# Two pooling projections computed as an eighth pair of seven block products, six left among the heads

## The chip, the cores and the metric

The kernel runs on one core of one Trainium2 chip. The metric is the device time of one execution in microseconds (us); of several runs the median is taken. The reader meets five engines of the core: PE (TensorE, the matrix unit, with its weight loads shown apart as PEld), DVE (VectorE), ACT (ScalarE), POOL (GpSimd) and SP (SyncE, which here only starts DMA transfers). Each engine takes its instructions in the order in which they stand in its own program, and an instruction waits on semaphores that other engines or DMA transfers raise.

## The reference

One layer of a streaming encoder on 512 tokens, model width 2048, eight heads of 128 channels, four pooling groups of 256 channels, feed-forward width 5632:

```python
h = rms_norm(x, pre_mix_g[l])
z = h @ w_in[l]
q = z[..., :ATTN_WIDTH].reshape(B, S, N_HEADS, HEAD_DIM)
k = z[..., ATTN_WIDTH:2 * ATTN_WIDTH].reshape(B, S, N_HEADS, HEAD_DIM)
v = z[..., 2 * ATTN_WIDTH:3 * ATTN_WIDTH].reshape(B, S, N_HEADS, HEAD_DIM)
u = z[..., 3 * ATTN_WIDTH:]
a = chunked_attention(q, k, v, rel_bias[l]).reshape(B, S, ATTN_WIDTH)
p = multiscale_pool(u, pool_w[l], pool_scale[l])
m = jnp.concatenate([a, p], axis=-1) @ w_o[l]
x = x + rms_norm(m, post_mix_g[l])
h = rms_norm(x, pre_ffn_g[l])
up = causal_dwconv(h @ w_up[l], conv_w[l], conv_b[l])
y = (jax.nn.gelu(up[..., :D_FF], approximate=True) * up[..., D_FF:]) @ w_down[l]
x = x + rms_norm(y, post_ffn_g[l])
```

The pooling takes u, 1024 channels: group g (256 channels) is averaged over a trailing window of 2, 4, 8 or 16 tokens, the token itself is subtracted, and the result goes through a 256x256 map and a scale per channel. The change concerns where the first 256 channels of u are computed, and when their pooling is done.

## The kernel before

**Numbers and tiles.** Activations lie transposed, channels on the 128 partitions and the 512 tokens along the row. Every float32 operand is split into a high part and a low rest (`split`: ACT rounds to the high part at L140, DVE subtracts at L141), and a product is three matmuls: high by high, high by low, low by high (`mm3`, L162, L164, L165). PE is where most of the time goes; its order is the order of the code, laid out by hand. The orders of DVE, ACT, POOL and SP are laid out by a scheduler when the program is built, from the same code.

**Stages, in us from the start of the span.** To 73: q and k of head 0, the first half of v. 73 to 205: q and k of heads 1 to 7, one head after the other (the "pairs"). 205 to 267: heads 0, 1, 2 among the second half of v. 267 to 388: the pooling projections u0 to u7 with heads 3 to 7 among them. 388 to about 545: the output projection. From there to the end: the feed-forward part.

**The pairs** (class `Pairs`, L440; `qk_product`, `qk_keep`). The q block and the k block of a head, two blocks of 128 output channels over 2048 input channels, are cut into halves of the input channels and of the tokens; the two by two product of blocks is made with seven block products instead of eight, in the order 1, 2, 5, 3, 6, 7, 4. Each of them is eight 128x512 matmuls (L170) and eight 128x256 matmuls (L176) through `mm2`. The weights come in four raw tiles of 128x1024 per pair (`load`, from `w_qk`); sums of raw tiles are made by DVE (L476 to L482), and each is split by ACT and DVE. The two 128x512 results of a pair go to DRAM as `zqk[h]` (L583).

**The heads.** `ready_head(h)` multiplies the reloaded pair `zq` by RR (the norm factors, with the sign of the second block turned, L668) and splits it into `qkh`, `qkl`; `scores(h)` is 12 matmuls on PE into `s`, then a softmax on DVE and ACT in four row blocks: scale and bias (L699), maximum (L702), exponential (ACT, L704), reciprocal (L706), scaling (L707). `turn(h)` transposes it on PE (L718, ten matmuls into `pt`) and splits the transposed tiles; `values(h)` multiplies by v. For heads 0 to 2 the loop `for h in range(3)` puts steps of the second half of v between these (`run`, 12 matmuls each).

**The pooling.** `project` computes one block u*j* with 48 matmuls of 128x512 from two weight tiles `u_0`, `u_1`; halfway through it a step of a head can be put in (`between`, made by `mid`). `pool_keep` (L732) multiplies the block by the norm factors (L736), makes the window sums (L740, as `us`), divides and subtracts (L745 to L748, as `tmp`), and splits the result (`dh`, `dl`). `pool_mix` (L750) is the 256x256 map: 12 matmuls into `pm`, stored to DRAM as `pooled` (L771) and later loaded again into `mixT` (L831).

**Queues and buffers around the change.** SP starts loads in its own order, each after the buffer it writes has been let go. `raw4` is a ring of five raw tiles of 128x1024 float32, `w4` a ring of eight split tiles (four pairs), and PSUM, where PE writes, has eight banks. At the end of the pairs, after block product 7 of the last pair, `restore` runs, and then `zq0` (the reloaded pair of head 0, L606) and `bias0` (L608) are started, both in `raw4` tiles. `more_sums(n)` starts DMA sums of feed-forward weights on POOL's queue, paced through these stages.

Of the kernel before, what the change touches and what calls it, by code (L numbers as in the profile page):

```python
# [9 lines left out]
F32 = mybir.dt.float32  # L10
# [5 lines left out]
P = 128  # L16
S = 512
# [4 lines left out]
HEADS = 8  # L22
# [59 lines left out]
def encoder_layer(ctx: ExitStack, tc: tile.TileContext, x, xT, vecs, rel, post_mix, post_ffn,  # L82
# [192 lines left out]
    specs += v_specs(1)  # L275
    for g in range(4):
        specs += u_specs(2 * g)
        if g:
            specs += pm_spec(g - 1)
        specs += u_specs(2 * g + 1)  # L280
# [98 lines left out]
    vd = [dram.tile([P, NT, 512], F32, name=f"vd{i}") for i in range(2)]  # L379
    pooled = dram.tile([P, 6, S], F32, name="pooled")  # L380

    z0 = raw4("z0").rearrange("p (a b) -> p a b", a=2)
# [58 lines left out]
    class Pairs:  # L441
# [3 lines left out]
        def __init__(self):  # L445
            n = self.n = HEADS - 1
            place_of = {1: 0, 2: 2, 5: 4, 3: 6, 6: 8, 7: 10, 4: 12}
            begin = [(0, 1), (0, 2), (0, 5), (1, 1), (0, 3)]
            order = [(k, i) for _, k, i in sorted((7 * k + at, k, i) for k in range(n) for i, at in place_of.items())]
            self.order = begin + [at for at in order if at not in begin]  # L450
            self.order.insert(-2, (None, None))
            self.raw, self.made, self.loaded, self.used = {}, [], 0, 0

        def load(self, k, i):
            def raw(what, tile_, m, kh):
                load_w.last = nc.sync.dma_start(tile_, w_qk[k + 1, m, kh]).ins
                self.raw[k, what] = tile_
# [99 lines left out]
    def qk_keep(k, i):  # L557
# [18 lines left out]
        elif i == 4:  # L576
# [5 lines left out]
            nc.vector.tensor_add(z[:, 0, T:], a[:, :T], z[:, 0, T:])  # L582
            nc.sync.dma_start(zqk[k + 1], z)  # L583

# [8 lines left out]
    for k, i in [at for at in pairs.order if at[0] is not None]:  # L593
# [9 lines left out]
        if (k, i) == (pairs.n - 1, 7):  # L603
            restore()
            state["z", 0] = raw4("zq0").rearrange("p (a b) -> p a b", a=2)
            nc.sync.dma_start(state["z", 0], zqk[0])  # L606
            state["bias", 0] = raw4("bias0")[:, :S]
            restore.last = nc.sync.dma_start(state["bias", 0], rel[0]).ins  # L608
        if i in (3, 7, 4) and k < pairs.n - 1:
            more_sums(1)  # L610
# [10 lines left out]
    with tc.tile_pool(name="p1", bufs=2, reuse_waits="tile") as p1:  # L621
# [21 lines left out]

        def project(name, between=None):
            ps = bank(name)
            for i in range(2):
                if i and between:
                    between()
                w = weights.get(f"{name}_{i}")
                for j in range(8):  # L650
                    kb = 8 * i + j
                    mm3(ps, part(w, j), g_both(hT, kb), kb == 0, kb == KD - 1)
            return ps
# [77 lines left out]

        def pool_keep(g, j, ps):  # L732
            w = WINDOWS[g]
            u = p1.tile([P, WIDE], F32, tag="u", bufs=1, name="u")[:, :PAD + S]
            nc.vector.memset(u[:, :PAD], 0.0)
            nc.vector.tensor_mul(u[:, PAD:], ps, R)  # L736
            cur, step = u, 1
# [40 lines left out]
        for h in range(3):  # L778
# [11 lines left out]
            run(1)  # L790
            ready_head(h + 1)
            run(1)
            turn(h)
# [5 lines left out]
        def mid(h):  # L799
            def step():  # L800
                values(h)
                if h == 2:
                    scores(3)
                elif h + 2 < HEADS:
                    ready_head(h + 2)
# [4 lines left out]

        for j in range(8):
            ps = project(f"u{j}", mid(2 if j == 0 else j + 1) if j not in (1, 7) else None)
            if j == 0:
                ready_head(4)
            if j == 2:
                v_ready()
            if 1 <= j <= 5:
                turn(j + 2)
                if j < 5:
                    scores(j + 3)  # L820
            if j in (2, 4, 6):
                pool_mix(j // 2 - 1, spill_mix)
# [998 lines left out]
```

## Time and profile before

| | us |
|---|---|
| median of three runs | 1853.03 |
| lowest, highest of the three | 1850.68, 1853.16 |
| the profiled execution | 1848.83 |
| its span | 1847.1 |
| PE busy | 1836.0 (99%) |
| DVE busy | 1465.3 (79%) |
| ACT busy | 1123.2 (61%) |
| POOL busy | 310.2 (17%) |

The span is what the profiler's records cover; the execution's own time is 1.7 us longer. A matmul's busy time of 0.39 us is not its cost: matmuls are pipelined, and a 128x512 matmul follows the one before it by about 0.23 us. A row of the timeline reads: start, busy time, engine, line, operation, out<-in by the program's names (numbers left out), shape, count, and in brackets how long the engine was idle before it and what ended that.

### The profile page before, as it was taken

The page shows a single profiled execution, that of the slowest core. Times are in us where ns is not written, and L with a number is a line of the kernel's source. Part 1 is how long each engine was busy: PE and PEld are TensorE (multiplying, and loading weights), DVE is VectorE, ACT ScalarE, POOL GpSimd, SP SyncE. Part 2 cuts the span into 40 slices and gives each one's busy share as a digit, 9 for nine tenths or more (in the row PEclk, how much of TensorE's full clock was granted, in tenths as well). Part 3 has the DMA queues.
Part 4 walks back from the last instruction along what each step waited for, and adds up shares of the span by engine and source line. Part 5 has one row for each costly group of instructions (what it writes and reads, how often), then busy time and mean ns, then how long its engine had stood idle before and what let it go on. Part 6 is the DMA issues. An engine that isn't in the chain of part 4 may idle for free.

```text
span 1847.1 us, 25323 instructions
## 1 busy us (share of the span) xinstructions
PE 1836.0 (99%) x9530; PEld 1577.9 (85%) x9530; DVE 1465.3 (79%) x1702; ACT 1123.2 (61%) x1486; POOL 310.2 (17%) x411
## 2 busy tenths in 40 slices
PE   9999999999999999999999999999999999999998
PEld 7888888888888888888888888888888888888886
DVE  6988778878679887777777777777777899899876
ACT  7655555457587666666666666666665655655553
POOL 3411000100001222222122222221221001111101
PEclk9999999999999999999999999999999999999999
DMA  8599978998979988988889888888888977787785
GB/s 320 173 319 301 319 228 234 277 262 305 336 283 283 248 211 206 208 198 202 206 205 198 204 201 207 195 208 206 203 175 303 360 216 166 195 217 175 176 243 145
DMA packets 139467, 430.21 MB, mean 233 GB/s; under 512 B 12048, under 2 KB 15504, under 8 KB 133648
## 3 DMA queue, kind: packets, MB, share of 16 engines
q0 software_dynamic: 56016, 177.75, 47.3%
q1 hardware_dynamic: 83328, 250.84, 38.6%
q8 instruction: 75, 1.23, 0.3%
q14 instruction: 48, 0.39, 0.1%
HBM read 374.54 MB, written 104.33 MB: 259 GB/s over the span
## 4 chain that ended last, share of the span: by engine, by line
PE 93%; DMA 3%; issue 1%; DVE 1%; ACT 1%; SPq 0%; POOL 0%; DVEq 0%; POOLq 0%; ACTq 0%
PE qa L170 19%; PE qa L176 10%; PE qg L170 9%; PE qg L176 5%; PE qd L170 5%; PE pa L165 4%; PE pa L164 4%; PE pa L162 4%; PE qd L176 2%; PE m L164 2%; PE m L162 2%; PE m L165 2%; PE pg L165 2%; PE pg L164 2%; PE pg L162 2%; PE v L165 2%
## 5 line engine op out<-in xcount | busy, mean ns | idle before, releaser
L170 PE MATMUL qa<-gT,wfh 128*128 128x512 f32 x1200 | 300.4, 392 | 0.0
L141 DVE TENSOR_TENSOR wfl<-x,wfh 128x1024 fp32r<-128x1024 f32 x165 | 202.0, 1225 | 94.8 <-ACT wfh L140 78.9
L170 PEld LDWEIGHTS qa<-gT,wfh 128*128 128x128 f32 x1200 | 215.9, 189 | 38.7
L140 ACT ACTIVATE wfh<-x 128x1024 fp32r<-128x1024 f32 x165 | 174.3, 1056 | 79.8 <-PE qg L170 45.9
L1118 POOL DMA_DIRECT2D x<-in_w_up x125 | 107.2, 860 | 477.0 <-DVE wfl L141 461.6
L176 PE MATMUL qa<-gT,wfl 128*128 128x256 f32 x1200 | 168.0, 283 | 0.7 <-ACT m L1446 0.6
L176 PEld LDWEIGHTS qa<-gT,wfl 128*128 128x128 f32 x1200 | 157.8, 191 | 5.4 <-ACT m L1446 0.8
L170 PE MATMUL qg<-h,wfh 128*128 128x512 f32 x656 | 162.1, 389 | 0.0
L141 DVE TENSOR_TENSOR wfl<-wy,wfh 128x1024 fp32r<-128x1024 f32 x100 | 122.0, 1222 | 33.8 <-ACT wfh L140 31.7
L170 PEld LDWEIGHTS qg<-h,wfh 128*128 128x128 f32 x656 | 123.0, 188 | 25.4
L140 ACT ACTIVATE wfh<-wy 128x1024 fp32r<-128x1024 f32 x100 | 105.1, 1053 | 64.3 <-PE qd L170 49.8
L140 ACT ACTIVATE bh<-b 128x2048 fp32r<-128x2048 f32 x56 | 106.1, 1914 | 62.1 <-DVE b L1245 24.1
L141 DVE TENSOR_TENSOR bl<-b,bh 128x2048 fp32r<-128x2048 f32 x56 | 127.1, 2286 | 18.6 <-ACT bh L140 11.7
L162 PE MATMUL pa<-bh,ah 128*128 128x512 f32 x320 | 124.5, 389 | 0.0
L164 PE MATMUL pa<-bl,ah 128*128 128x512 f32 x320 | 124.5, 389 | 0.0
L165 PE MATMUL pa<-bh,al 128*128 128x512 f32 x320 | 124.5, 389 | 0.0
L170 PE MATMUL qd<-gT,wfh 128*128 128x512 f32 x400 | 99.1, 390 | 0.0
L176 PEld LDWEIGHTS qg<-h,wfl 128*128 128x128 f32 x656 | 89.5, 190 | 6.4
L176 PE MATMUL qg<-h,wfl 128*128 128x256 f32 x656 | 91.5, 282 | 0.0
L170 PEld LDWEIGHTS qd<-gT,wfh 128*128 128x128 f32 x400 | 74.7, 188 | 15.3
L170 PE MATMUL qa<-h,wfh 128*128 128x512 f32 x344 | 86.1, 392 | 0.0
L141 DVE TENSOR_TENSOR wfl<-wz,wfh 128x1024 fp32r<-128x1024 f32 x50 | 61.1, 1223 | 28.8 <-PE qa L170 26.8
(576 smaller groups left out, 4275.5 us busy)
## 6 DMA issues: line engine op xcount, KB each, us to landing
x<-in_w_up POOLq DMA_DIRECT2D x125, 512.0 KB, 6.1
b<-in_w_down SPq DMA_DIRECT2D x32, 1024.0 KB, 6.9
wt<-in_w_o POOLq DMA_DIRECT2D x24, 1024.0 KB, 14.9
wz<-in_w_up SPq DMA_DIRECT2D x43, 512.0 KB, 5.5
x<-in_w_up SPq DMA_DIRECT2D x43, 512.0 KB, 5.0
wy<-in_w_up SPq DMA_DIRECT2D x43, 512.0 KB, 3.9
wy<-in_w_up POOLq DMA_DIRECT2D x43, 512.0 KB, 6.6
sum<-part POOLq DMA_DIRECT2D x38, 512.0 KB, 6.8
```

The source lines that it names most:

```text
L140: rounded = nc.scalar.activation(hi, src, AF.Copy)
L141: rest = nc.vector.tensor_sub(lo, src, f32(hi))
L162: nc.tensor.matmul(ps, l[0], r[0], start=first, stop=False, skip_group_check=onto)
L164: nc.tensor.matmul(low, l[0], r[1], start=False, stop=False, skip_group_check=onto)
L165: nc.tensor.matmul(ps, l[1], r[0], start=False, stop=last, skip_group_check=onto)
L170: nc.tensor.matmul(ps, w[0][:, kb], pairs[kb][0], start=fresh and not kb, stop=last, skip_group_check=not fresh)
L176: nc.tensor.matmul(ps[:, sl], w[1][:, kb], pair[:, sl], start=False, stop=last, skip_group_check=not fresh)
L1118: nc.gpsimd.dma_start(self.raw[k, what], self.block(k, m, kh), accum_op=ALU.add)
```

## The change

The list of pairs gets blocks of its own: (loader of weights, place of the result). The first two channel blocks of the pooling weights are put in as pair number 4 of now eight, between those of heads 4 and 5; the result goes to a new DRAM tensor `zu`. The weight list loses the tiles of u0 and u1, and `pm0` stands ahead of `u2` in it. After `bias0`, a third `raw4` tile `zur` is loaded from `zu`. In the loop of heads 0 to 2, head 0 does `pool_keep` on the first half of `zur`, head 1 on the second, with the factors of `RR` since the second block carries the turned sign, and head 2 does `pool_mix(0)`. The projections left are u2 to u7. `project` takes a table from input block to step: inside u2 stand `scores(3)` and `ready_head(4)` after 4 of 16 input blocks and `values(2)` after 10; the later heads move one projection on in number, so that the last head's `values(7)` stands in the middle of u7, where it stood in the middle of u6.

```diff
-    for g in range(4):
+    specs += pm_spec(0)
+    for g in range(1, 4):
         specs += u_specs(2 * g)
-        if g:
+        if g > 1:
             specs += pm_spec(g - 1)
         specs += u_specs(2 * g + 1)
...
+    zu = dram.tile([P, 2, S], F32, name="zu")
...
-            n = self.n = HEADS - 1
+            self.blocks = [(lambda m, kh, h=h: w_qk[h, m, kh], zqk[h]) for h in range(1, HEADS)]
+            self.blocks.insert(4, (lambda m, kh: w_u[m, kh], zu))
+            n = self.n = len(self.blocks)
...
-                load_w.last = nc.sync.dma_start(tile_, w_qk[k + 1, m, kh]).ins
+                load_w.last = nc.sync.dma_start(tile_, self.blocks[k][0](m, kh)).ins
...
-            nc.sync.dma_start(zqk[k + 1], z)
+            nc.sync.dma_start(pairs.blocks[k][1], z)
...
             restore.last = nc.sync.dma_start(state["bias", 0], rel[0]).ins
+            state["zu"] = raw4("zur").rearrange("p (a b) -> p a b", a=2)
+            nc.sync.dma_start(state["zu"], zu)
...
-        def project(name, between=None):
+        def project(name, between):
             ps = bank(name)
             for i in range(2):
-                if i and between:
-                    between()
+                if 8 * i in between:
+                    between[8 * i]()
                 w = weights.get(f"{name}_{i}")
                 for j in range(8):
                     kb = 8 * i + j
+                    if j and kb in between:
+                        between[kb]()
                     mm3(ps, part(w, j), g_both(hT, kb), kb == 0, kb == KD - 1)
...
-        def pool_keep(g, j, ps):
+        def pool_keep(g, j, ps, r=R):
...
-            nc.vector.tensor_mul(u[:, PAD:], ps, R)
+            nc.vector.tensor_mul(u[:, PAD:], ps, r)
...
             ready_head(h + 1)
+            if h < 2:
+                pool_keep(0, h, state["zu"][:, h], RR[:, h, :])
+            else:
+                pool_mix(0, spill_mix)
             run(1)
             turn(h)
...
-                if h == 2:
-                    scores(3)
-                elif h + 2 < HEADS:
+                if 2 < h < HEADS - 2:
                     ready_head(h + 2)
...
+        def first_scores():
+            scores(3)
+            ready_head(4)
+
-        for j in range(8):
-            ps = project(f"u{j}", mid(2 if j == 0 else j + 1) if j not in (1, 7) else None)
-            if j == 0:
-                ready_head(4)
-            if j == 2:
+        for j in range(2, 8):
+            ps = project(f"u{j}", {8: mid(j)} if j > 2 else {4: first_scores, 10: mid(j)})
+            if j == 3:
                 v_ready()
-            if 1 <= j <= 5:
-                turn(j + 2)
-                if j < 5:
-                    scores(j + 3)
-            if j in (2, 4, 6):
+            if j < 7:
+                turn(j + 1)
+            if j < 6:
+                scores(j + 2)
+            if j in (4, 6):
                 pool_mix(j // 2 - 1, spill_mix)
```

The orders on the engines change at three places that matter below. In the rows, lines of the kernel after stand 4 to 8 higher than those of before for the same statement. What an engine's row waits for stands in brackets as the semaphore's name: DMAHW a DMA transfer, PE, DVE, Activation, Pool that engine.

DVE, at the start of head 0, before (`zq_2037` is `zq0`, `bias_2039` is `bias0`, `s_1` to `s_3` are PE's score banks):

```order
L668 TENSOR_TENSOR zq_2037<-zq_2037,RR 128x1024 [waits DMAHW1_49]
L141 TENSOR_TENSOR qkl<-zq_2037,qkh 128x1024 [waits Activation_49]
L141 TENSOR_TENSOR v_1l<-v_1r,v_1h 128x1024 [waits DMAHW7_49,PE_49,Activation_49]
L689 MEMSET bias_2039 64x64 [waits DMAHW2_49]
L699 SCALAR_TENSOR_TENSOR s<-s_1_2188,bias_2039 128x128 [waits DVE_49,PE_49]
```

And of the change, the same stretch:

```order
L676 TENSOR_TENSOR zq_2221<-zq_2221,RR 128x1024 [waits DMAHW6_49]
L744 TENSOR_TENSOR u<-zur,RR 128x512 [waits DMAHW2_49]
L748 TENSOR_TENSOR us<-u 128x527 [waits DVE_49]
L141 TENSOR_TENSOR qkl<-zq_2221,qkh 128x1024 [waits Activation_49]
L753 TENSOR_TENSOR uf<-us,recip 128x16 [waits DVE_49,Pool_49]
L756 SCALAR_TENSOR_TENSOR tmp<-us,u 128x496
L141 TENSOR_TENSOR v_1l<-v_1r,v_1h 128x1024 [waits DMAHW4_49,PE_49,Activation_49]
L697 MEMSET bias_2223 64x64 [waits DMAHW7_49]
L755 TENSOR_TENSOR tmp<-uf,u 128x16 [waits DVE_49]
L743 MEMSET u 128x16 [waits DVE_49]
L744 TENSOR_TENSOR u<-zur,RR 128x512
L141 TENSOR_TENSOR dl_2475<-tmp,dh_2474 128x512 [waits Activation_49]
```

The multiplication of `zur` by RR, which waits for the new load, and the first window sum now stand between the multiplication of `zq0` and the row that makes `qkl`; five more rows of the pooling stand between `qkl` and the softmax, whose first row (scale and bias) comes right behind the last row shown.

SP, where head 0's loads are started, before:

```order
L606 DMA zq_2037<-zqk_350 128x1024 [waits DMAHW2_49,DMAHW1_49,DVE_49]
L608 DMA bias_2039<-in_rel 128x512 [waits DMAHW4_49,DVE_49,Activation_49]
L658 DMA bias<-in_rel 128x512 [waits DMAHW3_49,PE_49]
L658 DMA bias<-in_rel 128x512
L152 DMA v_2r<-in_w_v 128x1024 [waits DMAHW5_49,DVE_49]
```

And of the change:

```order
L610 DMA zq_2221<-zqk_350 128x1024 [waits DMAHW7_49,DMAHW6_49,DVE_49]
L612 DMA bias_2223<-in_rel 128x512 [waits DMAHW1_49,DVE_49,Activation_49]
L666 DMA bias<-in_rel 128x512 [waits DMAHW0_49,PE_49]
L666 DMA bias<-in_rel 128x512
L614 DMA zur<-zu 128x1024 [waits DMAHW2_49,DVE_49]
L152 DMA v_2r<-in_w_v 128x1024 [waits DMAHW3_49,DVE_49]
```

The load of `zur` stands fifth, where `v_2r` stood, in the ring place that `v_2r` had; what both wait for on DVE is the end of `v_7l`, the split of the weight tile that held that place. `v_2r` comes one later.

PE, at the end of the loop of heads 0 to 2, before (`v_3h` is a weight tile of v, `v_2`, `v_3` are banks, `u_2655` is the bank of u0):

```order
L162 MATMUL v_3_1974<-v_3h,gT_136 128x512
L164 MATMUL v_3_1974<-v_3l,gT_136 128x512
L165 MATMUL v_3_1974<-v_3h,gT_136 128x512
L718 MATMUL pt_0_2626<-ident,s 128x128 x4
L718 MATMUL pt_1_2627<-ident,s 128x128 x4
L718 MATMUL pt_2_2628<-ident,s 128x128 x2
L162 MATMUL u_2655<-gT_135,u_0h 128x512
```

And of the change, the step ahead of that same last step of v:

```order
L162 MATMUL pm_1_2843<-dh_2474,pm0h 128x512
L164 MATMUL pm_1_2843<-dl_2475,pm0h 128x512
L165 MATMUL pm_1_2843<-dh_2474,pm0l 128x512
L162 MATMUL pm_1_2843<-dh_2660,pm0h 128x512
L164 MATMUL pm_1_2843<-dl_2661,pm0h 128x512
L165 MATMUL pm_1_2843<-dh_2660,pm0l 128x512
L162 MATMUL v_0_2155<-v_3h,gT_136 128x512
```

The twelve matmuls of `pool_mix(0)`, of which the last six are shown, moved from the middle of the projections to a place ahead of the last step of v in the loop; after the transposes of head 2 comes u2 where u0 was.

## The prediction

> **What bounds the kernel now.** I read the page first: the busy times and the clock by slices.
>
> ```profile
> PE 1836.0 (99%) x9530; PEld 1577.9 (85%) x9530; DVE 1465.3 (79%) x1702; ACT 1123.2 (61%) x1486; POOL 310.2 (17%) x411
> PEclk9999999999999999999999999999999999999999
> ```
>
> PE is busy for 1836.0 of 1847.1 us at full granted clock, so time falls only if PE gets less to do, and rises wherever PE is made to wait. What there is to gain is decided by PE's work, what there is to lose by how close the other engines run behind it. So next the windows by stage (start:end, length, then busy time of PE, PEld, DVE, ACT, POOL, the clock, the DMA share and GB/s):
>
> ```profile
> 105.00:124.50 19.50, 19.50 (x114) 17.23 (x113) 17.63 (x23) 10.97 (x14) 1.87 (x6) 1.00 1.06 352
> 205.00:267.00 62.00, 62.00 (x313) 52.84 (x312) 48.04 (x101) 34.22 (x66) 3.07 (x8) 1.00 0.84 274
> 267.00:388.00 121.00, 121.00 (x601) 103.01 (x600) 95.01 (x224) 60.46 (x115) 16.02 (x30) 1.00 0.92 254
> 320.00:342.00 22.00, 22.00 (x114) 18.93 (x113) 20.24 (x52) 12.21 (x25) 4.22 (x8) 1.00 1.00 252
> ```
>
> PE never waits in a pair (first row), in the heads with v (second) or in the projections (third). DVE is at 17.63 of 19.50 in that pair and at 20.24 of 22 in the densest piece of the projections (fourth): it has little to spare, and that is where a rearrangement can hurt.
>
> **What the change removes on PE.** The timeline of PE gives the length of a pair and of a projection.
>
> ```profile
> 104.91 0.86 PE L170 MATMUL qa<-gT,wfh 128*128 128x512 f32 x3
> 182.88 0.63 PE L170 MATMUL qa<-gT,wfh 128*128 128x512 f32 x2
> ...
> 282.24 0.39 PE L162 MATMUL u<-gT,u_0h 128*128 128x512 f32 x1
> 293.12 0.93 PE L718 MATMUL pt<-ident,s 128*128 128x128 f32 x7
> ```
>
> The first two rows are the same place in pairs that lie four apart: 182.88 - 104.91 = 77.97, or 19.49 us for a pair. The second two are the start of u1, whose 48 matmuls stand alone, and the first instruction behind it: 293.12 - 282.24 = 10.88 us. Two projections, 21.76, become one pair, 19.49: **2.27 us less on PE**, 0.12% of the whole. The pair brings its own splits, sums and loads, but the rows of seven pairs show that PE waits for none of them, and its weights are the bytes that u0 and u1 loaded. New are a store and a load of 512 KB. Nothing else can be won: the same matmuls of heads, v and pooling map are in both.
>
> **What it puts in the way of head 0.** The order of DVE has `pool_keep(0, 0)` begin ahead of `qkl`, the split that the scores of head 0 need. The stretch before, from DVE, ACT and PE:
>
> ```profile
> 215.06 1.22 DVE L141 TENSOR_TENSOR v_7l<-v_7r,v_7h 128x1024 fp32r<-128x1024 f32 x1
> ...
> 220.04 1.23 DVE L668 TENSOR_TENSOR zq<-zq,RR 128x1024 f32<-128x1024 f32 x1 [1.29 <-DMA zq<-zqk]
> 222.39 1.22 DVE L141 TENSOR_TENSOR qkl<-zq,qkh 128x1024 fp32r<-128x1024 f32 x1 [1.13 <-ACT qkh L140]
> 223.54 1.22 DVE L141 TENSOR_TENSOR v_1l<-v_1r,v_1h 128x1024 fp32r<-128x1024 f32 x1
> ...
> 225.28 0.62 DVE L699 SCALAR_TENSOR_TENSOR s<-s,bias 128x128 f32<-128x128 f32 x2 [0.46 <-PE s L165]
> ...
> 230.16 1.23 DVE L141 TENSOR_TENSOR v_2l<-v_2r,v_2h 128x1024 fp32r<-128x1024 f32 x1 [1.04 <-ACT v_2h L140]
> ...
> 233.61 0.49 DVE L707 TENSOR_SCALAR s<-s,rs 128x512 f32<-128x512 f32 x1
> ```
>
> ```profile
> 224.37 0.28 PE L162 MATMUL s<-qkh 128*128 128x256 f32 x1
> 234.49 1.26 PE L718 MATMUL pt<-ident,s 128*128 128x128 f32 x10
> ```
>
> `qkl` is done at 223.61 and PE takes up the scores at 224.37: 0.8 us to spare. The softmax is done at 234.10 and the transposes begin at 234.49; only the fourth of ten reads the last row block, 3 x 0.1 us on, so 0.7 us to spare. All times here are in the time of before; in the changed kernel the whole stretch lies a pair later.
>
> Now `zur`. Its load takes the place of `v_2r` on SP and in the ring, and both wait for the end of `v_7l`, at 216.28. The rows of SP, and the landing times of loads of the same size (512 KB), of `v_2r`, of `zq`, and of `u_1r`:
>
> ```profile
> 206.69 0.33 SPq L606 DMA_DIRECT2D zq<-zqk  x1
> ...
> 216.31 0.33 SPq L152 DMA_DIRECT2D v_2r<-in_w_v  x1
> 216.69 0.42 SPq L663 DMA_DIRECT2D zq<-zqk  x1
> ```
>
> ```profile
> DMA to landing us min/median/max: 7.8/7.8/7.8
> ```
>
> ```profile
> DMA to landing us min/median/max: 4.4/8.6/13.3
> ```
>
> ```profile
> DMA to landing us min/median/max: 3.9/5.9/8.0
> ```
>
> `v_2r` took 7.8 us from 216.31. The three `zq` are those started at 206.69 (13.3: it gave DVE its wait until 220.04), at 216.69 (8.6) and at 235.9 (4.4). I take 7.8, the load in the same place: `zur` is there at 216.31 + 7.8 = 224.1. The bounds are 3.9 and 13.3. What I can't see is how the sums on POOL's queue, which stand differently ahead of it, share the DMA engines.
>
> From the landing, DVE does the multiplication and one window sum before `qkl`. The rows of those, and of the rest of `pool_keep`, from the groups of the projection stage:
>
> ```profile
> L736 DVE TENSOR_TENSOR u<-u,RR 128x512 f32<-128x512 f32 x8 | 5.5, 688 | 12.0 <-PE u L165 12.0
> L740 DVE TENSOR_TENSOR us<-u 128x527 f32<-128x527 f32 x8 | 5.5, 694 | 0.1
> L748 DVE SCALAR_TENSOR_TENSOR tmp<-us,u 128x496 f32<-128x496 f32 x7 | 4.7, 668 | 0.0
> L141 DVE TENSOR_TENSOR dl<-tmp,dh 128x512 fp32r<-128x512 f32 x7 | 4.8, 683 | 0.6 <-ACT dh L140 0.6
> ```
>
> Each holds DVE for some 0.6 us (a row overlaps its follower by under 0.1: 222.39 + 1.22 against 223.54). So `qkl` ends at 224.1 + 1.2 + 1.2 = 226.5, and PE waits from 224.37: **about 2.2 us at the scores**. Then DVE has, ahead of the softmax, `uf` 0.1, `tmp` 0.6, `v_1l` 1.15, three small rows 0.2, the second block's multiplication 0.6 and `dl` 0.6, 3.3 in all: the softmax starts at 229.8 instead of 225.28. It took 234.10 - 225.28 = 8.8 us, and gets 1.4 more of pooling (`us`, `uf`, `tmp` of the second block), which fits into gaps of 1.04 ahead of `v_2l` and about 0.5 in an earlier gap, all but some 0.3: done at 238.9. That is 4.8 late, less the 0.7 to spare: **4.1 us for head 0**, 2.2 at the scores and 1.9 at the transposes. In short the delay is the landing minus 220.0, and since DVE isn't through with `zq0` before 221.27, it doesn't fall below 1.2 on this order, however early `zur` is.
>
> At this place I weigh a rule. The Trainium skill, page "DMA: Bandwidth & Descriptors", section "Anatomy of one DMA — SWDGE (gpsimd) path", fits a DMA's time as about 2.0 us plus its bytes over 436 per ns, which for 512 KB would be an estimate of 3.2 us; by it `zur` would be there at 219.5 and the delay would be its least, 1.2 instead of 4.1. The two rows at this very place, 7.8 and 8.6, don't agree with it, and I stay with them.
>
> **What it puts in the way later.** Head 1: its transposes had 0.35 to 0.4 to spare, by
>
> ```profile
> 249.76 0.49 DVE L707 TENSOR_SCALAR s<-s,rs 128x512 f32<-128x512 f32 x1
> 250.43 1.26 PE L718 MATMUL pt<-ident,s 128*128 128x128 f32 x10
> ```
>
> (end 250.25, with the fourth transpose again later); `dl` of block 1 comes into that stretch with 0.7 and a split of the pooling weights stands where a wider one of u0 stood. Between 0 and 0.7, and I take 0.1, since the weight split takes most of it away. In the dense piece (20.24 of 22) a head now stands one projection earlier by name, with the same work around it: 0 to 0.5, I take 0.1; not below nothing, since PE doesn't wait there now. `mixT` is the third. Its load of the stored pooling results waits for the last head's output; the row of who waited, and the landing times of the pooled tiles:
>
> ```profile
>   DVE mixT L939: 4.9, 1
> ...
> DMA to landing us min/median/max: 5.8/7.3/11.0
> ```
>
> DVE waited 4.9 us for it, and PE didn't notice. Now `values(7)` stands in u7 rather than u6, so the load starts nearly a projection later, still ahead of the output projection's second factor. DVE's order has splits of output weights behind that wait: nothing at 5.8, about 1.2 at 11.0. I take 0.4. The weights' sums on POOL are paced by as many calls less one; it is off PE's way, and I take nothing, with 0.3 to either side.
>
> **The sum.** -2.27 + 4.1 + 0.1 + 0.1 + 0.4 = +2.4 us. The profiled execution took 1848.83 (span 1847.1), so 1851.2 in its terms. That execution is 4.2 us under the median of the three runs, 1853.03, so by the median **1855.4**.
>
> **The rivals.**
>
> *`zur` is early.* If the queue is emptier when `zur` starts (`u_1r`, 15 us later, took 3.9), it lands by 221.2 and head 0 costs 1.2. With the other terms near nothing that is -2.27 + 1.2 = -1.1: 1851.9. For it speaks that the sums running in that stretch stand otherwise than before; against it, that three loads between 206 and 217 took 7.8 to 13.3. The skill's fit above stands on this side.
>
> *`zur` is late: slower.* If it takes 13.3 like `zq0`, the last reload from DRAM ahead of it, it lands at 229.6, and head 0 waits 9.6: -2.27 + 9.6 + 0.6 = +7.9, or 1861.0. The mechanism is one: DVE stands at the multiplication of `zur`, with `qkl` behind it. It makes the kernel slower by more than 0.2% (3.7 us, about what a measurement of this kernel can tell from no change) once the wait reaches 5.4, that is from a landing of 9.1 us on. For it: `zq0` is a reload from DRAM, as `zur` is; against it: the next reload, in the same queue 0.4 us behind `v_2r`, took 8.6. In this case PE would stand for 7.7 us at once, and a clock row matters:
>
> ```profile
> 1838.00:1839.00 1.00, 0.75 (x7) 0.54 (x5) 0.76 (x4) 0.38 (x2) 0.00 (x0) 1.00 0.03 8
> 1843.00:1844.00 1.00, 0.00 (x0) 0.00 (x0) 0.60 (x2) 0.00 (x0) 0.00 (x0) 0.53 1.03 367
> ```
>
> After PE's last work, in the slice from 1838, the granted clock holds until about 1843 and then falls to half: some 4.3 us of standing. The waits of the forecast, 2.2 and 1.9 with scores between them, stay under that; 7.7 does not, and would cost up to half of the work done until the clock is back, which no row here shows. The Trainium skill, page "TensorE: Matmul & The Clock Gate", section "Part 1: The HAM clock gate", has the clock halved after an idle window of about 3.4 us and released after as much busy time, by which this case would be an estimated 1.7 us slower still, 1862.7; the row above agrees with the fall.
>
> *The dense places give way too.* Head 0 as forecast, and the three later terms at their upper ends, 0.7 + 0.5 + 1.2: -2.27 + 4.1 + 2.4 = +4.2, 1857.3. For it: DVE at 92% in the dense piece; against it: each has its own slack in before, and PE waits nowhere there.
>
> That the change doesn't do what it says I leave out: the eighth pair is the same code as the seven.
>
> **How the numbers follow.** Forecast 0.45, `zur` early 0.25, late 0.15, dense places 0.15. The predicted time is the forecast's, 1855.4. The range reaches from 1850.2, which leaves out the lower end of the early case (all of 2.27 gained, 1850.8, and a little luck), to 1861.0, which leaves out the upper part of the late one. The bound of 3.7 us gives 1849.3 and 1856.7: faster 0.06 (from the early case alone, by the spread of runs, 1850.68 to 1853.16), slower 0.32 (the late case, most of the dense one, and a sixth of the forecast), within 0.62.
>
> **What the profile after would show.** A pair more of 19.5 us with no wait of PE in it, and projections of 10.9 behind it. At head 0, a wait of DVE at the multiplication of `zur`, ended by its DMA; a wait of PE of about 2.2 at the scores, ended by DVE's `qkl`, and one of about 1.9 at the first transposes, ended by DVE's scaling. The landing of `zur` near 7.8. If PE waits nowhere at head 0, the forecast is wrong and the early case holds; if it waits for 5 or more at the scores, the late one. If PE waits at the transposes of heads 1 to 5, or at the output projection for a split of its weights, the later terms were too small. If the eighth pair is longer than 19.5, the gain was wrong.

## The result, and the profile after

| | before | after |
|---|---|---|
| median of the runs on one chip, us | 1852.38 (4 runs) | 1861.63 (4 runs) |
| lowest to highest, us | 1850.68 to 1853.16 | 1858.88 to 1862.47 |
| ratio, 95% interval | | 1.0053 [1.0041, 1.0065] |
| the profiled execution, us | 1848.83 | 1858.88 |
| its span, us | 1847.1 | 1857.1 |

The kernel became slower by 9 us, 0.5%, where the forecast was 1855.4 and the range ended at 1861.0. The first page of the profile after: busy time and share by engine, and PE's granted clock.

```profile
PE 1836.4 (99%) x9546; PEld 1577.9 (85%) x9546; DVE 1474.9 (79%) x1716; ACT 1129.5 (61%) x1494; POOL 311.1 (17%) x413
PEclk9999999989999999999999999999999999999999
```

PE's busy sum hardly moved: the 2.27 us that the pair saves are about what slow matmuls at a low clock add (2.5, below). One slice of the clock, the ninth (371 to 418 us), now shows an 8. The waits of PE in the profile after (what PE waited for, total us, times, longest):

```profile
PE m L162 <- ACT wo_3h L140: 6.2, 1, 6.2
PE m L164 <- DVE wo_3l L141: 1.9, 1, 1.9
PE pt L726 <- DVE s L715: 1.1, 1, 1.1
PE pd L162 <- ACT ah L140: 1.1, 1, 1.1
...
PE pd L165 <- DVE al L141: 0.5, 1, 0.5
```

None of these five is among the waits of before, and none is at the scores of head 0 (`s <- qkl`) or at its transposes. The windows of after show where (columns as in the prediction):

```profile
105.00:203.00 98.00, 98.00 (x564) 86.53 (x563) 81.90 (x104) 49.92 (x60) 16.54 (x32) 1.00 1.04 305
388.00:436.00 48.00, 39.83 (x166) 32.15 (x165) 34.52 (x39) 24.42 (x29) 1.15 (x1) 0.89 0.89 279
```

The five pairs of the first row run without a gap. In the second, the output projection, PE stands for 8.2 of 48 us at a mean clock of 0.89; before, it was busy for all 48:

```profile
388.00:436.00 48.00, 48.00 (x214) 39.74 (x213) 42.96 (x50) 28.83 (x34) 0.00 (x0) 1.00 0.93 303
```

**How that loss comes about.** The chain of work that ended last in 372 to 411, of after (start, length, what):

```profile
377.20 11.13 DMA pooled<-mx
...
388.36 0.37 SPq L152
...
388.77 12.11 DMA mixT<-pooled
...
400.91 1.23 DVE mixT L951
...
404.49 1.16 DVE wo_3l L141
...
405.69 0.80 PE m L164
```

Two transfers take 23 of the 28 us from 377.20 to 405.69: the third store of pooling results (`pooled`, L779), and the load of all stored results into `mixT` (L843). The timeline of SP, of after and then of before, shows how the one came to stand behind the other:

```profile
377.20 0.34 SPq L779 DMA_DIRECT2D pooled<-mx  x1
377.89 0.37 SPq L152 DMA_DIRECT2D wo_1r<-in_w_o  x1
388.36 0.37 SPq L152 DMA_DIRECT2D wo_2r<-in_w_o  x1
388.77 0.93 SPq L843 DMA_DIRECT2D mixT<-pooled  x2
```

```profile
370.70 0.34 SPq L831 DMA_DIRECT2D mixT<-pooled  x1
371.14 0.38 SPq L152 DMA_DIRECT2D wo_3r<-in_w_o  x1
...
380.45 0.34 SPq L771 DMA_DIRECT2D pooled<-mx  x1
```

Before, the first half of `mixT` was loaded at 370.70, ten us ahead of the third store. After, `values(7)`, whose end lets that load's buffer go, stands in u7 and ends at 382.9. By then SP holds at `wo_2r`, a weight tile that takes over the ring place of `mx`, the tile that the store reads. So a load that could have gone at 382.9 waits until the store has landed at 388.3. It lands at 400.9, and two engines have stood still in front of it, each with a split of `wo_3` behind (`wo_3` is the fourth weight tile of the output projection; the names `wo_0` to `wo_3` come round again every four tiles). The timelines of DVE and ACT of after:

```profile
400.91 1.23 DVE L951 TENSOR_TENSOR mixT<-mixT,mixT 128x1024 f32<-128x1024 f32 x1 [14.83 <-DMA mixT<-pooled]
```

```profile
400.91 1.06 ACT L140 ACTIVATE a<-mixT 128x1024 fp32r<-128x1024 f32 x1 [16.08 <-DMA mixT<-pooled]
```

PE needed `wo_3h` at 396.56 (its timeline, of after; 396.33 plus 0.23):

```profile
396.33 0.39 PE L165 MATMUL m<-wo_2h,a 128*128 128x512 f32 x1
402.97 0.79 PE L162 MATMUL m<-wo_3h,a 128*128 128x512 f32 x1 [6.24 <-ACT wo_3h L140]
405.69 0.80 PE L164 MATMUL m<-wo_3l,a 128*128 128x512 f32 x1 [1.93 <-DVE wo_3l L141]
...
406.71 0.63 PE L162 MATMUL m<-wo_3h,a 128*128 128x512 f32 x1
407.14 0.63 PE L164 MATMUL m<-wo_3l,a 128*128 128x512 f32 x1
...
409.94 0.39 PE L162 MATMUL m<-wo_0h,a 128*128 128x512 f32 x1
```

The 12 matmuls of `wo_3` should have ended at 396.56 + 12 x 0.227 = 399.28; `wo_0h` begins at 409.94, 10.7 us later. Of these, 6.24 + 1.93 = 8.17 are waits, and nearly all of the other 2.5 is the clock: after 6 us of standing it was at half, a matmul takes 0.63 to 0.80 instead of 0.39, and they follow each other by 0.43 instead of 0.23.

**The sum.** -2.27 (the pair) + 10.7 (output projection) + 1.15 (transposes of head 5, `pt`) + 1.15 + 0.53 (`pd`, first product of the down projection) = +11.3, and the spans differ by 10.0. Waits of 0.5 and 0.6 us that only the profile of before has, at `q` and in the feed-forward part, account for most of the rest.

### The profile page after: what moved, and what is told of

Read it like the earlier page. It is cut to its first block, busy times and chain, and to the rows that moved or that the text cites. A ratio compares the mean times of both kernels' runs of the same rounds, so it can differ in the third digit from the quotient of the medians.

```text
span 1857.1 us, 25403 instructions
## 1 busy us (share of the span) xinstructions
PE 1836.4 (99%) x9546; PEld 1577.9 (85%) x9546; DVE 1474.9 (79%) x1716; ACT 1129.5 (61%) x1494; POOL 311.1 (17%) x413
## 4 chain that ended last, share of the span: by engine, by line
PE 96%; DMA 2%; DVE 1%; ACT 0%; issue 0%; SPq 0%; DVEq 0%; POOLq 0%; ACTq 0%
PE qa L170 20%; PE qa L176 11%; PE qg L170 10%; PE qg L176 5%; PE qd L170 5%; PE pa L164 4%; PE pa L165 4%; PE pa L162 4%; PE m L164 3%; PE m L165 3%; PE qd L176 3%; PE m L162 3%; PE pg L164 2%; PE pg L165 2%; PE pg L162 2%; PE v L164 2%
## 5 line engine op out<-in xcount | busy, mean ns | idle before, releaser
L170 PE MATMUL qa<-gT,wfh 128*128 128x512 f32 x1224 | 306.4, 392 | 0.0
L170 PEld LDWEIGHTS qa<-gT,wfh 128*128 128x128 f32 x1224 | 220.2, 189 | 39.5
```

The source lines that it names most:

```text
L170: nc.tensor.matmul(ps, w[0][:, kb], pairs[kb][0], start=fresh and not kb, stop=last, skip_group_check=not fresh)
```

## The experiments

The theory: the loss sits in the chain store, `mixT` load, splits of `wo_3`, and it is there because SP's order puts the load behind the store. The rivals: DVE and ACT are too slow there whatever the load does; the half clock is what costs; head 0 costs what was predicted and something else hides it. Each edit is made on the kernel after, and each ratio is to before on the same chip. "Waits in `m`" are PE's waits in the output projection.

### The load ahead of the weights on SP

```diff
-        for n, sl in ((2, slice(0, 4)), (3, slice(0, 2))):
-            nc.sync.dma_start(mixT[n][:, sl, :], pooled[...])
+        load_w.behind = nc.sync.dma_start(mixT[2], pooled[:, :4, :]).ins
+        nc.sync.dma_start(mixT[3][:, :2, :], pooled[:, 4:, :])
```

`load_w.behind` makes every later weight load stand behind the first half's load.

> The loads of the output weights from the fifth on are put behind the load of mixT's third tile on SP; nothing else is changed. Theory (queue): in the changed kernel that load could start at 382.9 but stood behind a weight load that waited for the third store of pooled (11.1 us to land) and started at 388.8. Here it starts near 383, lands 8 to 12 us later, at 391 to 395, and PE's wait at the third weight tile of the output projection (6.2 + 1.9) falls to 0 to 3, with no fall of the clock: 8 to 10.5 us faster than the changed kernel, 1851 to 1854. Rival (the place of values(7)): the queue doesn't matter because the load lands no earlier than 395 anyway: gain of at most 6 us, a wait of 2 or more left. Rival (the load's own length): the load takes longer the earlier it starts, landing stays near 400, no gain.

Measured 1.0024 [1.0009, 1.0039]. SP's timeline of this kernel:

```profile
382.56 0.34 SPq L845 DMA_DIRECT2D mixT<-pooled  x1
387.78 0.32 SPq L846 DMA_DIRECT2D mixT<-pooled  x1
388.19 0.39 SPq L153 DMA_DIRECT2D wo_1r<-in_w_o  x1
```

The load starts at 382.56, as soon as `values(7)` allows, and lands in 9.1, at 391.7. Waits in `m` fall from 8.2 to 4.0 us, and by the two ratios about half of the slowdown goes. Of the 4.0, 2.0 are still at `wo_3`, behind the landing. Another 1.2 are at the splits of later tiles: their weights start only at 388.2, behind the second half's load, which must wait for the store.

### Weight splits ahead of the wait

```diff
+        if name == "wo1_1_2":
+            round_w.third = split.last, split.rest
...
-        a12 = wo_left("a12", 1, 0)
+        with tc.issue_after(round_w.third[0]), tc.issue_after(round_w.third[1]):
+            a12 = wo_left("a12", 1, 0)
```

The subtraction at L951 is held back in the same way. The load stays late. `wo1_1_2` is the seventh weight tile, so in this kernel's timelines ACT and DVE split four tiles, the fourth to the seventh, before what waits for `mixT`; in after they split none of these first.

> ACT and DVE get the splits of the first seven weight tiles of the output projection ahead of the two operations that wait for mixT (the split a12 and the subtraction); the load itself is as late as in the changed kernel (start near 388.8, landing near 400.9). Theory: PE waited only because these operations stood ahead of the third tile's split; a12 is not needed before the second product, near 413, so no wait of PE at 397 and none later: 10 us faster than the changed kernel, near 1851. Rival: the late load is needed anyhow, and PE waits at the second product instead: 0 to 5 us faster.

Measured 1.0037 [1.0025, 1.005]; waits in `m` 5.9, the longest now 2.5 at `a12` itself. By the waits that is less than the earlier load gives (4.0); in time the two intervals overlap. Work that is moved ahead of the wait comes free, but what depends on `mixT` is as late as before.

### PE kept busy through the wait

```diff
+                if (i, cc, q) == (1, 0, 3):
+                    for n in range(29):
+                        nc.tensor.matmul(wo_banks[7], w[0][:, n % 2, :P], w[0][:, n % 2], start=True, stop=True)
```

29 matmuls whose result is thrown away stand where PE waits for `wo_3`.

> 29 matmuls of 128x512 whose result is thrown away are put into PE's order where the changed kernel waits for the third weight tile (6.6 us of work). Theory: the wait costs 8.2 us plus about 2.3 us of half clock behind it (11 matmuls at 0.43 instead of 0.23 us); with PE kept busy through the first wait, the matmuls behind follow at 0.23 and the kernel is 2 us faster than the changed one, near 1859.5. Rival: the slow matmuls have another cause (weights arriving late), then it is the same, 1861.6, or slower by what the filler adds.

Measured 1.0081 [1.006, 1.0101], not faster, rather slower than after. `wo_0h` begins at 408.61 instead of 409.94: the clock held, and the matmuls behind followed each other by 0.23. Then PE had to wait for DVE (its timeline):

```profile
418.39 0.57 PE L164 MATMUL m<-wo_2l,a 128*128 128x512 f32 x1 [3.96 <-DVE wo_2l L141]
```

So 1.3 of the 2.5 us came back, and were lost again at a split of DVE that is late here and not in after. DVE's timelines show why: the scheduler gave this kernel another order, with three `mixT` rows and the split of `s` (411.85 to 417.12) ahead of the split of `wo_2`, which starts at 417.12; in after it starts at 411.57. So this run changes two things, and doesn't price the clock alone. That the clock is not the whole loss follows from after itself: 8.17 of the 10.7 are waits.

### The last head's values earlier

```diff
-            ps = project(f"u{j}", {8: mid(j)} if j > 2 else {4: first_scores, 10: mid(j)})
+            ps = project(f"u{j}", {4 if j == 7 else 8: mid(j)} if j > 2 else {4: first_scores, 10: mid(j)})
```

> values(7) stands after 4 instead of 8 input blocks of u7, 2.7 us earlier; the scheduler then also puts the load of mixT's third tile ahead of the weight load that waits for the store. Theory: load starts near 380.5, lands at 389 to 393, no wait of PE at the third weight tile: near 1851. Rival (the load takes 12 us and the waits ahead of the splits decide): landing near 393 leaves a wait of up to 1.5 us: 1852.5.

Measured 1.0039 [1.0025, 1.0052]; waits in `m` 4.6. SP's timeline:

```profile
380.61 8.19 SPq L843 DMA_DIRECT2D mixT<-pooled  x2
388.85 0.43 SPq L152 DMA_DIRECT2D wo_2r<-in_w_o  x1
```

The first load goes at 380.61, 8.2 us sooner than in after, but takes 15.8 us and lands at 396.4, only 4.5 sooner. The second load holds SP until the store has landed (8.19 us in this row of two loads). So the load's own length counts as well as its start.

### A buffer of its own for the third store

```diff
-                state["mx"] = raw4("mx").rearrange("p (a b) -> p a b", a=2)
+                state["mx"] = (p1.tile([P, 2, S], F32, tag="zq", bufs=1, name="zq") if kb == 12 else
+                               raw4("mx").rearrange("p (a b) -> p a b", a=2))
```

With that no weight load waits for the store.

> The third result of the pooling map goes to DRAM out of the tile that zq no longer needs, instead of out of a tile of the weight ring. So no weight load waits for that store to land; all else is as in the changed kernel. Theory (one cause for the queue and the late weights): SP comes to the load of mixT's third tile at 383 instead of 388.8, and the output weights' seventh tile doesn't start late; it lands at 391 to 392, PE waits 1 to 3 in all in the output projection (8.2 in the changed kernel, 4.2 and more in the run with SP's order alone): 5 to 7 us faster than the changed kernel, some 2 to 4 over before. Rival (the operations that wait for mixT ahead of the splits are what matters, not the store): no better than the run with SP's order alone, over 4 above before.

Measured 1.0027 [1.0016, 1.0039]; the load starts at 383.52, waits in `m` are 3.6. That confirms what held SP: it was the place of `mx` in the ring. But the load takes 13.0 and lands at 396.5, so about half of the slowdown stays with the queue free.

### No third store

```diff
+                if h == 7:
+                    mixT.extend(acc8(f"mixT{i}", "B").rearrange("p (a b) -> p a b", a=4) for i in (2, 3))
+                    pool_mix(2, keep_mix)
...
-            if j in (4, 6):
-                pool_mix(j // 2 - 1, spill_mix)
+            if j == 4:
+                pool_mix(1, spill_mix)
```

The third group goes straight into `mixT` after `values(7)`; one load of 1 MB is left, put ahead of the output weights on SP from the sixth tile on.

> pool_mix(2) is moved behind values(7) in u7 and writes its result into mixT directly: no third store, no load of mixT's fourth tile, and the weights are put behind the load of the third. Theory: the load starts near 383 with less beside it and lands by 391; the wait for it still stands ahead of the third split on DVE, so PE waits 0 to 2 there: within 0 to 3 us of before. Rival: moving pool_mix(2) holds up the pooling's buffers (dh, dl) and PE waits in u7 or at pm3: 3 or more over before.

Measured 1.0001 [0.9991, 1.0011]. The load starts at 379.74 and lands in 8.3, at 388.0; waits in `m` are 1.3. The slowdown is gone, so DVE and ACT are not too slow there once the load is early. The edit does more than take the store away: with the twelve matmuls of `pool_mix(2)` behind it, `values(7)` ends at 379.7 instead of 382.9, and the second load is gone too. How much each gives was not separated.

### Combinations

The first two edits together:

> The first two edits together (weights behind the load on SP; splits ahead of what waits for mixT on ACT and DVE), the third store left. Theory: what is left of the two single runs (waits of 4.2 and 5.9 in the output projection) came from the one that the other removes and from weights whose ring tile the store holds until 388: 1 to 3 of wait are left: 1 to 3 over before. Rival: the two gains are the same gain, and 4 are left.

Measured 1.0033 [1.0018, 1.0047], no better than the first alone; waits in `m` 4.3. Of the tiles that are to be split first, the sixth (`wo_1` in the row) now lands only at 400.7, 12 us after its start at 388.65, and ACT and DVE stand for it (DVE's timeline):

```profile
401.75 1.23 DVE L141 TENSOR_TENSOR wo_1l<-wo_1r,wo_1h 128x1024 fp32r<-128x1024 f32 x1 [6.56 <-ACT wo_1h L140]
```

No third store, and the split first:

> No third store, the load ahead of the weights, and the splits ahead of what waits for it. Theory: no wait of PE in the output projection; the pair's gain of 2.3 stands against a wait of 0.5 to 1.1 at one head's transposes and of 1.7 at the first down product, which all runs of the changed kernel show: within 1 us of before, 1850 to 1852. If the gain of 2.3 were not there, 2 over before.

Measured 0.9999 [0.9988, 1.001]. PE stands nowhere in the window in which after lost 8.2 us:

```profile
388.00:436.00 48.00, 48.00 (x214) 39.75 (x213) 44.68 (x49) 31.34 (x35) 1.15 (x1) 1.00 1.00 313
```

### The waits at the down projection

1.15 and 0.53 us at `pd` stand in after and in every variant so far, 1000 us behind the change, in code that the change doesn't touch. ACT's row there, of after and of before:

```profile
1433.05 1.06 ACT L140 ACTIVATE ah<-gc 128x1024 fp32r<-128x1024 f32 x1 [8.73 <-PE pa L165]
```

```profile
1421.90 1.06 ACT L140 ACTIVATE ah<-gc 128x1024 fp32r<-128x1024 f32 x1 [5.43 <-DMA gc<-gd]
```

Before, `ah` waits for its input; after, for PE's product `pa`, which is no input of it. The theory: the eighth pair takes split tiles out of the rings, the tiles that follow fall on other places of the memory, and `ah` is now written where a tile lay that `pa` still reads. To test that, two unused split tiles are taken at that place, touched by a POOL memset of one column, first on the kernel without the third store and with the split first, then on the kernel after:

```diff
             nc.sync.dma_start(v, gd[0][0][:, :, 0, :])
+            for _ in range(2): nc.gpsimd.memset(f32(w4("pad"))[:, :1], 0.0)
```

> The three edits of the output projection as before, and two dummy tiles of the split ring (one column written by POOL) ahead of the first left factor of the down projection, so that its low part no longer lies where the second left factor's high part is written. Theory: the waits of 1.1 and 0.5 at the first down product, which all profiles of the changed kernel show and that of before does not, come from that place in SBUF: ACT's split there had to wait for PE's second product. They go: 1.7 faster than the run with the three edits alone, and 1 to 2 faster than before. Rival: the split waits for the reload gc instead (13.7 us to land), and nothing is gained.

> Only the two dummy tiles, in the changed kernel. Theory: 1.7 faster than the changed kernel, all else as it is: 7 to 9 over before. Rival: 9 to 10 over before.

Measured 1.0014 [1.0005, 1.0023] and 1.0073 [1.0058, 1.0089]. The wait for `ah` went, but POOL now stood ahead of loads of the down weights, for 8.06 us at the first memset and 1.80 at the second, waiting for PE, and a longer wait came in its place (waits of PE, of the first of the two):

```profile
PE pd L169 <- DMA bl<-rw02l: 2.4, 1, 2.4
```

So the test was spoiled by its own means. The clean one only exchanges two buffers in the order in which they get their places:

```diff
-        for r in (..., later["wl"], scratch, slot_h, slot_l):
+        for r in (..., later["wl"], slot_h, scratch, slot_l):
```

> Only that exchange, in the changed kernel. Theory: the waits at the first down product go, all else stays: 1.7 faster than the changed kernel, 7 to 8.5 over before. Rival: no change, 9 to 10 over before.

Measured 1.0042 [1.0028, 1.0056]. The windows from 1430 on, of after and of this kernel:

```profile
1430.00:1845.00 415.00, 413.33 (x1823) 341.61 (x1822) 355.01 (x257) 236.65 (x243) 46.79 (x45) 1.00 0.79 215
```

```profile
1430.00:1845.00 415.00, 415.00 (x1833) 343.63 (x1832) 355.01 (x256) 236.60 (x243) 47.30 (x46) 1.00 0.79 217
```

The 1.7 us are gone in the profile, so the place of the buffers makes that wait; which tile lay where is not on record. In the ratio the two intervals overlap, so the time alone doesn't show it.

### Head 0, with a late `zur`

`zur` is loaded twice (the first load, from `zqk[0]`, is overwritten), so that it lands later, and its multiplication by RR is forced ahead of `qkl`.

```diff
+            nc.sync.dma_start(state["zu"], zqk[0])
             nc.sync.dma_start(state["zu"], zu)
...
+                with tc.issue_after(pool_keep.first):
+                    split.rest = nc.vector.tensor_sub(pair[1], v, f32(pair[0])).ins
```

> In the changed kernel zur is loaded twice, the second load behind the first one's landing, and the multiplication of zur is kept ahead of qkl on DVE, so that what the prediction feared happens: zur some 4 to 8 us later, at 243.5 to 248 instead of 239.7. By the prediction's formula with the measured zero (no delay at 239.7), PE waits by about the landing minus 240.5 in all, at the scores (landing + 1.9 - 243.4) and at the transposes: 3 to 7 us, and the kernel is so much slower than the changed one: 12 to 16 over before. Rival: the scores of head 0 have more room than the formula says, because the gap that DVE had ahead of qkl and the slack at the transposes take it up: under 1.5 of wait.

Measured 1.0082 [1.0068, 1.0096]. DVE's and PE's timelines:

```profile
245.41 0.69 DVE L800 TENSOR_TENSOR u<-zur,RR 128x512 f32<-128x512 f32 x1 [2.22 <-DMA zur<-zu]
```

```profile
247.30 0.41 PE L164 MATMUL s<-qkl,qkh 128*128 128x256 f32 x1 [3.51 <-DVE qkl L684]
```

With a late `zur` the wait at the scores is there: 3.5 us, which is the landing, 245.4, plus the 1.9 to the end of `qkl`, less the 243.8 at which PE is ready. There is no wait at head 0's transposes. The prediction's formula, landing less 220.0 (239.0 in the time of after), gives 6.4 for this landing: it is 2.9 too high. 1.9 of that is the part at the transposes, which does not occur; some 0.6 is the window sum, which stands behind `qkl` in this kernel. The span is 5.5 longer than that of after (1862.6 against 1857.1), not 3.5: behind the wait the granted clock is at half from about 247.5 to 250.9, some 1.7 us more, as much as the prediction's late rival put on it (1862.7 against 1861.0).

### A version faster than both

No third store, the split first, and the two buffers exchanged:

> The three edits of the output projection, and in the feed-forward part the first place of the left factors' ring exchanged with that of a scratch tile, with no dummy tile and nothing on POOL. Theory: the dummy tiles of the run before took the wait of ACT's split away but put two POOL instructions ahead of four loads; without them the waits of 1.1 and 0.5 at the first down product go and no wait for a load comes: 1.7 faster than the three edits alone, 1 to 2 faster than before. Rival: the split waits for the reload gc (13.7 us), or the scratch tile takes over the wait: no gain, same as before.

Measured 1849.38 (11 runs) against 1852.73: 0.9980 [0.9969, 0.9991], faster than before by 1.7 to 5.7 us. Its profiled run, 1853.45, was its slowest and shows waits of 1.6, 0.9, 0.9, 0.7 and 0.3 in `m`; ACT stood there for weights (5.7 and 2.3 us for two `wo_2` tiles). The variant without the exchange had 0.5 there. What the faster ten runs did in that place no profile shows, and the intervals of the two versions touch, so the gain of the exchange alone is not shown in time.

## Why the prediction was wrong

**The step that failed is the third of "what it puts in the way later": `mixT`.** It was put at 0.4, with 1.2 as its upper end, and measured 10.7. The prediction said that "the load starts nearly a projection later, still ahead of the output projection's second factor", and then priced its landing by the times of before (5.8 to 11.0 us). Of these the 11.0 is no load: it is the third store itself, started at 380.45; the two loads of `mixT` took 5.8 and 7.3. The load landed at 400.9 instead of 376.5, 24.4 us later: 12.3 because `values(7)` ends later, which was foreseen, 5.9 in the queue, and 6.3 because the transfer took 12.1 instead of 5.8. Three things were missing.

- *What the load is moved past on SP.* `values(7)` ends 12 us later, and by then the third store is on its way and a weight load that waits for the store's tile stands ahead. That gives 5.9 of the lateness (388.8 against 382.9). The edits that free the load from the queue take about half of the slowdown away (1.0024 and 1.0027), and the one without the store and with an earlier `values(7)` all of it (1.0001). It could have been read in the order of SP: in before `mixT` stands ahead of `wo_3r` and of the store, in after behind the store and `wo_2r`.
- *How long the load takes there.* 1 MB took 5.8 us in before, 12.1 in after together with the second load, 13.0 and 15.8 where it was started earlier and the third store was still on its way, and 9.1 in that same place with the later weight loads held behind it. What shares the DMA engines with it was not taken apart.
- *What is behind the wait on two engines.* ACT and DVE stood for 16 and 15 us, from 384.8 and 386.1 to 400.9, with `wo_3`'s splits behind them, and PE needed the first of these at 396.56. Before, DVE's wait of 4.9 us was hidden because the first split behind it was due 10 us after its end (DVE's and PE's timelines, of before):

```profile
376.48 1.23 DVE L939 TENSOR_TENSOR mixT<-mixT,mixT 128x1024 f32<-128x1024 f32 x1 [4.87 <-DMA mixT<-pooled]
...
378.22 1.22 DVE L141 TENSOR_TENSOR wo_0l<-wo_0r,wo_0h 128x1024 fp32r<-128x1024 f32 x1
```

```profile
389.69 0.39 PE L162 MATMUL m<-wo_0h,a 128*128 128x512 f32 x1
```

The landing moved by 24.4 us, which is more than that cover.

The half clock, 2.5 of the 10.7, wasn't in that term at all. And the error at head 0 (below) hid part of this one: with head 0 at nothing the prediction's sum is -1.7, against +10.0 by the spans.

**The pair: right.** The five pairs between two rows of PE, of after:

```profile
106.46 1.91 PE qa L176 x16
...
203.92 1.91 PE qa L176 x16
```

97.46 / 5 = 19.49 us, as predicted, with no wait in the pairs.

**Head 0: 4.1 predicted, nothing measured.** The rows of DVE, of after:

```profile
239.66 0.69 DVE L744 TENSOR_TENSOR u<-zur,RR 128x512 f32<-128x512 f32 x1 [0.75 <-DMA zur<-zu]
...
241.01 1.22 DVE L141 TENSOR_TENSOR qkl<-zq,qkh 128x1024 fp32r<-128x1024 f32 x1
```

`zur` landed 4.3 us after its start, not 7.8. In all the profiles with the unchanged load it was 3.3 to 4.5, so this wasn't chance; why the tile in the same place before took 7.8 is not settled. By the fit of the Trainium skill, page "DMA: Bandwidth & Descriptors", section "Anatomy of one DMA — SWDGE (gpsimd) path", an estimate of 3.2 us, `zur` would have been early, and there it was nearer than the neighbouring rows, although the section is about DMAs that POOL issues and SP started this one. For the transfers that decided, it is no help: it gives an estimated 3.2 for the store, which took 11.1, and 4.4 for 1 MB of `mixT`, which took 5.8 in before and 8.0 to 9.7 in the versions without the third store.

The least delay of 1.2 wasn't there either. The prediction quoted that DVE stood for 1.13 us ahead of `qkl`, waiting for ACT's `qkh`, and yet added the two pooling rows in full: they fit into that gap and the 0.8 to spare. `zq0` was also ready sooner: its multiplication starts 5.7 us ahead of the scores in after (237.70, 243.40), 4.3 in before. The rule behind it, a late `zur` delays the scores, holds: 3.5 us in the run with two loads. Its part at the transposes doesn't.

**The dense piece: 0.1 predicted, 1.1 measured** (0.3 to 1.0 in the other profiles of the change). The windows of after:

```profile
324.00:336.00 12.00, 12.00 (x59) 10.08 (x58) 11.98 (x31) 8.90 (x20) 1.28 (x2) 1.00 1.09 230
336.00:348.00 12.00, 10.85 (x58) 9.13 (x57) 11.39 (x31) 6.47 (x14) 2.12 (x5) 1.00 0.91 319
```

DVE has no time left there (11.98 of 12). No run was made to take that wait away.

**The down projection: not foreseen.** 1.7 us, from the places of buffers.

**The rivals.** "`zur` is early" held at head 0, and would have given 1851.9. "`zur` is late" gave 1861.0, close to the measured time by chance, since its mechanism did not occur. "The dense places give way too" named `mixT`, with a ninth of its price. Its reason against, that PE waits nowhere there, was read in before, where the load was ten us ahead of the store.

## What to carry to other kernels

When a step moves later, list what its transfers now stand behind on their queue, and when the buffers of *those* come free: here a load whose data had long been stored waited behind a weight load that waited for another tile's store. An engine that waits is priced by what stands behind it in its order and when that is due; a wait that PE didn't notice before was hidden up to some 10 us, and the change moved its end by 24. A range of transfer times must hold transfers of the same kind: the upper end here was the store that stood in the way. And a gap that is quoted must also be used in the sum: two DVE rows that fell into one cost nothing.

## What the runs showed of the hardware

- The granted clock fell after shorter standing than the 4.3 us that the end of before had shown. In after, PE's last matmul ended at 396.7, and the windows are

```profile
398.00:399.00 1.00, 0.00 (x0) 0.00 (x0) 0.00 (x0) 0.00 (x0) 0.73 (x1) 0.97 0.87 363
399.00:400.00 1.00, 0.00 (x0) 0.00 (x0) 0.00 (x0) 0.00 (x0) 0.41 (x1) 0.50 1.01 412
...
408.00:409.00 1.00, 1.00 (x4) 0.81 (x3) 1.00 (x3) 0.00 (x0) 0.00 (x0) 0.50 0.45 130
409.00:410.00 1.00, 1.00 (x6) 0.79 (x5) 1.00 (x3) 0.00 (x0) 0.00 (x0) 0.91 0.79 246
```

  It fell about 2.2 us after PE's last work, and came back near 409.2, 3.5 us after PE was steadily busy. In the run with the splits ahead of the wait, it fell at the end of a wait of 2.5; in the run with earlier values, it held through one of 2.8 and fell in the next. So no fixed length of standing decides, and above 2.2 none is safe in these runs. The Trainium skill, page "TensorE: Matmul & The Clock Gate", section "Part 1: The HAM clock gate (the "warmup" mystery)", has the clock halved after at least one idle window of about 3.4 us, in windows that run freely. That the length varies, from 2.2 to 4.3, fits windows that run freely; a fall after 2.2 or 2.5 is sooner than one whole window, and there the measurement differs from the Trainium skill.
- The third store, 512 KB, took 11.13 us (11.0 in before), and `zur`, a load of the same size, 4.3. Beside the store, sums on POOL's queue and weight loads run; which of them it shares the DMA engines with was not taken apart.
